# Where a stretch of 256 bytes begins: moving the transposed activations of a two-layer trunk by 128 bytes in SBUF

## The chip, the cores and the metric

The kernel runs on one core of one Trainium2 chip. The metric is the device time of one execution in microseconds (us), lower is better. The engines are named as the profile names them: PE is TensorE's matrix multiply, PEld its weight load, DVE is VectorE, ACT is ScalarE, POOL is GpSimd and SP is SyncE, whose queue issues most of the DMAs.

## The reference, cut to what matters

Two layers over 512 tokens of width 1024, in float32. Each layer is a mixer and a gated MLP, both with an RMS norm ahead and behind:

```python
for l in range(DEPTH):                         # 2
    h = rms_norm(x, norm_mix_pre[l])
    proj = h @ w_in[l]                         # 1024 x 2560
    ...                                        # attention, retention, pooling heads
    mix = jnp.concatenate([o_da, o_ret, o_pool], axis=-1) @ w_out[l]   # 1024 x 1024
    x = x + rms_norm(mix, norm_mix_post[l])
    h = rms_norm(x, norm_mlp_pre[l])
    y = conv_mlp(h, w_up[l], conv_w[l], conv_b[l], w_down[l])          # 1024 x 5632, 2816 x 1024
    x = x + rms_norm(y, norm_mlp_post[l])
```

## The kernel before

Every large product is computed from split operands. A float32 tile is written as a high part plus a low remainder, both in the type `float32r`, and each product is three matmuls: high by high, high by low and low by high. A matmul holds a 128x128 block as the stationary operand (loaded by a weight load of its own) and streams up to 512 columns of the other operand, the moving one, past it. In a row of the profile such as `ps_m<-ht,wb` the moving operand stands first and the stationary one second.

The weights come in units of 128x1024 elements: a DMA into a `raw` tile (three buffers), then a split by ACT (L272, L283) and DVE (L273, L284) into a pair `wa`, `wb` (six pairs) or, for the last units of a stage, into `space`, which is room of the tiles `U1` and `U2` that are free by then.

The activations are kept transposed, features on the partitions. The tile `ht` holds the transposed, split residual stream: 8 feature chunks, each with a high and a low row of 512 tokens, 32 KB in each partition. The tiles `c1`, `c2`, `c3h`, `c3l`, `c4h` and `c4l` (shown as `c`, `c3h` and so on) hold other split activations in the same manner: the mixer's output, and in the MLP a part of the gated values. `xs` is the residual stream itself, `cst` the constants, `par` the parameters of the layer.

A layer passes four stages, in this order on PE:

- In (w_in, five slices of 512 columns): in the first four, tokens are the output's rows, so the stationary operand is a block of `ht` and the moving one a weight tile (`wa,ht`). In the fifth, features are the rows: `ht` moves, the weights stand still (`ht,wa`). The attention and the retention are put in between by a table of due times, as short matmuls and transposes on the same PE.
- Out (w_out): stationary `c` tiles, moving weights (`wa,c`), still with retention and pooling in between.
- Up (w_up, eleven groups of four feature blocks): `ht` moves, weights stand still. The first group and part of the second are done in halves of 256 columns, the rest in full 512.
- Down (w_down, 22 chunks of 128 features, for each chunk 4 token blocks of 6 matmuls = 24 matmuls): weights move. The stationary operand is a `c` tile for chunks 0 to 7, `ht` (by then free for reuse) for chunks 8 to 15, and a `c` tile again for chunks 16 to 21.

By the loops, the matmuls of 512 columns that use `ht` number, in both layers together: 768 with `ht` standing and 192 with it moving in the In stage, 1872 with it moving in Up, 384 with it standing in Down. Another 480 in Up move 256 columns of `ht`.

Where the tiles lie: a pool gives the tiles of SBUF their bytes one behind the other, each tag at its first use. Ahead of the pools lie 16,384 bytes that are reserved and four small constants of 32 bytes each, so the first tile begins 128 bytes into a stretch of 256. The first is `cst`, then `xs`, `ht`, `par`, `rt` and the rest. Two lengths are rounded up by `up_to_lines`, those of `cst` and `par`:

```python
up_to_lines = lambda n: -(-n // 32) * 32
...
cst = one.tile([P, up_to_lines(NCONST)], F32, tag="cst", name="cst")
...
xs = one.tile([P, NT, D], F32, tag="xs", name="xs")
ht = one.tile([P, KC, 2, S], F32R, tag="ht", name="ht")
...
t = one.tile([P, up_to_lines(NPAR)], F32, tag="par", name=nm("par"))
```

`cst` gets 1152 words (4608 bytes, 18 stretches of 256) and `par` 480 words (1920 bytes, 7.5 stretches), so `cst`, `xs`, `ht` and `par` begin at byte 128 of a stretch, and every large tile behind `par` at byte 0. The lines that issue the matmuls and the transposes are two helpers, L319 (`mm`) and L322 (`tr`).

Of the kernel before, what the change touches and what calls it, by code (L numbers as in the profile page):

```python
# [11 lines left out]
F32 = mybir.dt.float32  # L12
# [8 lines left out]
P = 128  # L21
# [64 lines left out]
    _n += _w  # L86
NCONST = _n

up_to_lines = lambda n: -(-n // 32) * 32

_PAR_PARTS = [("gmix", 8), ("gmlp", 8), ("subln", 1), ("retn", 2), ("pools", 2), ("conv", 44 * 4), ("pw", 256)]
_PAR_AT = {}
# [44 lines left out]
def tile_trunk(ctx: ExitStack, tc: tile.TileContext, x, xt, win, wout, wup, wdown, gpost, par, lam, const, out):  # L137
# [3 lines left out]
    one = ctx.enter_context(tc.tile_pool(name="one", bufs=1))  # L141
# [10 lines left out]
    def nm(s):  # L152
        uid[0] += 1
        return f"{s}_{uid[0]}"
# [21 lines left out]
    def rot_tmp():  # L176
        return one.tile([P, 512], F32, tag="rt", name=nm("rt"))

    cst = one.tile([P, up_to_lines(NCONST)], F32, tag="cst", name="cst")
    def C(name):  # L180
        lo, hi = _CONST_AT[name]
        return cst[:, lo:hi]
# [954 lines left out]
```

## Time and profile before

| | |
|---|---|
| median of 3 runs | 1173.18 us (1172.22 to 1174.98) |
| the profiled execution's own time | 1173.23 us |
| its span, first to last instruction | 1171.4 us |
| PE busy | 1153.6 us (98%), 5472 matmuls |
| DVE busy, ACT busy | 742.1 us (63%), 549.1 us (47%) |
| mean granted TensorE clock | 0.999 |

The profiled execution stands 0.05 us from the median. Matmuls are pipelined, so that the duration in a matmul's row overlaps with the next matmul's. How fast PE works through a stage is read from the starts: the chain of work that ended last gives for each piece its start, its length from there to the next piece's start, and the number of instructions in it.

### The profile page before, as it was taken

Reading aid. Unit: us, or ns where it says so; the run is one execution under the profiler, and the core shown is the slowest. Engines: PE = TensorE matmul, PEld = TensorE weight load, DVE = VectorE, ACT = ScalarE, POOL = GpSimd, SP = SyncE. Lnnn points to the kernel's source line nnn. Section 1 sums busy time; section 2 is a strip of 40 time slices with the busy share of each in tenths; the row PEclk is TensorE's granted clock in tenths of the full one; section 3 lists DMA queues with packets and bytes.
Section 4 is the critical chain, followed back from the end, with each engine's and each line's share of the span. In section 5 each row is a group of like instructions: output and inputs, shape, how many; then the busy total and the mean of one; then the engine's idle time right before and its main releaser. Section 6 shows DMA issues by size and latency. Waiting matters only on the chain.

```text
span 1171.4 us, 14837 instructions
## 1 busy us (share of the span) xinstructions
PE 1153.6 (98%) x5472; PEld 945.5 (81%) x5472; DVE 742.1 (63%) x1668; ACT 549.1 (47%) x1049; POOL 12.5 (1%) x21
## 2 busy tenths in 40 slices
PE   9999999999999999999999999999999999999997
PEld 6788777988888888888888887789888888888885
DVE  5988696776556547422777896876856645663224
ACT  5966553564444335312467754454645434452211
POOL 1000000000000000000000000000000000000000
PEclk9999999999999999999999999999999999999999
DMA  8411131332222322324023111313332222223311
GB/s 316 132 60 64 55 104 45 109 126 90 97 102 76 105 91 100 105 90 144 1 96 120 56 66 42 108 40 121 113 103 93 85 96 97 102 74 107 98 46 55
DMA packets 31321, 109.22 MB, mean 93 GB/s; under 512 B 3729, under 2 KB 4241, under 8 KB 31249
## 3 DMA queue, kind: packets, MB, share of 16 engines
q1 hardware_dynamic: 29952, 105.12, 26.4%
q10 hardware_dynamic: 1296, 3.16, 0.8%
q8 instruction: 43, 0.70, 0.2%
q14 instruction: 30, 0.24, 0.1%
HBM read 106.16 MB, written 2.10 MB: 92 GB/s over the span
## 4 chain that ended last, share of the span: by engine, by line
PE 91%; DVE 4%; ACT 2%; DMA 2%; issue 1%; SPq 0%; DVEq 0%; ACTq 0%
PE ps_m L319 52%; PE ps_s L319 18%; PE ps_b L319 9%; PE ps_o L319 9%; PE ps_b L322 2%; DMA raw<-in_wout 1%; ACT t L686 1%; DMA raw<-in_wup 1%; ACT wa L283 0%; DVE space L284 0%; DVE ks L623 0%; DMA raw<-in_win 0%; PE ps_m L322 0%; DVE sm L378 0%; DVE wb L284 0%
## 5 line engine op out<-in xcount | busy, mean ns | idle before, releaser
L319 PE MATMUL ps_m<-ht,wb 128*128 128x512 f32 (+1 forms) x768 | 201.6, 371 | 0.0
L319 PE MATMUL ps_m<-ht,wa 128*128 128x512 f32 (+1 forms) x768 | 200.0, 368 | 0.0
L284 DVE SCALAR_TENSOR_TENSOR wa<-raw,par,wa 128x512 fp32r<-128x512 f32 x128 | 95.6, 747 | 157.4 <-ACT wa L283 157.2
L283 ACT ACTIVATE wa<-raw,par 128x512 fp32r<-128x512 f32 x128 | 92.1, 720 | 198.2 <-PE ps_m L319 97.9
L319 PEld LDWEIGHTS ps_m<-ht,wb 128*128 128x128 f32 x768 | 135.0, 188 | 26.7 <-issue 1.0
L319 PEld LDWEIGHTS ps_m<-ht,wa 128*128 128x128 f32 x768 | 135.1, 188 | 25.6 <-issue 1.0
L319 PE MATMUL ps_m<-wa,ht 128*128 128x512 f32 x512 | 151.4, 403 | 0.6 <-ACT wa L283 0.6
L319 PE MATMUL ps_m<-wb,ht 128*128 128x512 f32 x448 | 131.0, 398 | 0.0
L319 PEld LDWEIGHTS ps_m<-wa,ht 128*128 128x128 f32 x512 | 94.9, 191 | 21.5 <-ACT wa L283 1.5
L273 DVE TENSOR_TENSOR wb<-raw,wa 128x1024 fp32r<-128x1024 f32 x38 | 46.6, 1226 | 84.9 <-ACT wa L272 84.9
L284 DVE SCALAR_TENSOR_TENSOR wb<-raw,par,wb 128x512 fp32r<-128x512 f32 x128 | 95.6, 747 | 4.7 <-ACT wb L283 4.6
L319 PEld LDWEIGHTS ps_m<-wb,ht 128*128 128x128 f32 x448 | 82.8, 189 | 17.5
L283 ACT ACTIVATE wb<-raw,par 128x512 fp32r<-128x512 f32 x128 | 91.9, 720 | 4.1 <-PE ps_m L319 3.4
L272 ACT CAST wa<-raw 128x1024 fp32r<-128x1024 f32 x38 | 39.8, 1048 | 89.6 <-PE ps_m L319 81.3
L319 PE MATMUL ps_s<-ht,wb 128*128 128x512 f32 (+1 forms) x264 | 70.7, 376 | 0.0
L319 PE MATMUL ps_s<-ht,wa 128*128 128x512 f32 (+1 forms) x264 | 70.2, 374 | 0.0
L319 PE MATMUL ps_m<-wa,c 128*128 128x512 f32 x224 | 65.6, 399 | 1.3 <-DVE pooled L666 1.3
L319 PEld LDWEIGHTS ps_s<-ht,wb 128*128 128x128 f32 x264 | 47.3, 188 | 10.1
L319 PEld LDWEIGHTS ps_s<-ht,wa 128*128 128x128 f32 x264 | 47.6, 188 | 9.8
L319 PEld LDWEIGHTS ps_m<-wa,c 128*128 128x128 f32 x224 | 41.6, 188 | 11.3 <-DVE pooled L666 2.2
L686 ACT ACTIVATE t<-ps_s,sm 128x128 f32<-128x128 f32 (+3 forms) x64 | 33.5, 527 | 21.4 <-DVE sm L684 18.5
L1007 ACT ACTIVATE t<-ps_m,par 128x512 f32<-128x512 f32 x48 | 36.4, 772 | 12.9 <-PE ps_m L319 12.9
(314 smaller groups left out, 1888.1 us busy)
## 6 DMA issues: line engine op xcount, KB each, us to landing
raw<-in_wup SPq DMA_DIRECT2D x88, 512.0 KB, 3.4
raw<-in_wdown SPq DMA_DIRECT2D x44, 512.0 KB, 3.4
raw<-in_win SPq DMA_DIRECT2D x39, 512.0 KB, 3.7
raw<-in_wout SPq DMA_DIRECT2D x16, 512.0 KB, 3.5
xs<-in_x SPq DMA_DIRECT2D x4, 512.0 KB, 9.5
gain<-in_gpost ACTq DMA_DIRECT2D x4, 512.0 KB, 4.3
t<-in_xt SPq DMA_DIRECT2D x3, 512.0 KB, 6.8
out<-xs SPq DMA_DIRECT2D x4, 256.0 KB, 2.0
```

The source lines that it names most:

```text
L272: se.copy(h, r)
L273: ve.tensor_tensor(out=lo, in0=r, in1=h.bitcast(F32), op=ALU.subtract)
L283: se.activation(a, x, AF.Copy, scale=sc)
L284: ve.scalar_tensor_tensor(b, x, sc, a.bitcast(F32), op0=ALU.mult, op1=ALU.subtract)
L319: in_order(te.matmul(out, lhsT=lhsT, rhs=rhs, **k))
L322: in_order(te.transpose(out, in_, ident))
L686: se.activation(p[:, 0:n], sb[:, 0:n], AF.Exp, bias=top, accum_out=sums[:, m:m + 1])
L1007: se.activation(acc, ps, AF.Identity, bias=conv[:, f, 3:4], scale=conv[:, f, 2:3])
```

## The change

The unit of `up_to_lines` becomes 64 words (256 bytes), and ahead of `cst` a tile of 32 words (128 bytes) is placed that nothing reads or writes.

```diff
-up_to_lines = lambda n: -(-n // 32) * 32
+STRETCH = 64
+up_to_lines = lambda n: -(-n // STRETCH) * STRETCH
...
+    one.tile([P, STRETCH // 2], F32, tag="edge", name="edge")
     cst = one.tile([P, up_to_lines(NCONST)], F32, tag="cst", name="cst")
```

`par` becomes 512 words long; `cst` stays at 1152. The first byte of the tiles in each partition, from the built programs:

| tile | before | within 256 | after | within 256 |
|---|---|---|---|---|
| cst | 16512 | 128 | 16640 | 0 |
| xs | 21120 | 128 | 21248 | 0 |
| ht | 37504 | 128 | 37632 | 0 |
| par | 70272 | 128 | 70400 | 0 |
| rt | 72192 | 0 | 72448 | 0 |
| U1 (ks, act, space) | 74240 | 0 | 74496 | 0 |
| c1 | 107008 | 0 | 107264 | 0 |
| wa, the first | 141824 | 0 | 142080 | 0 |
| raw, the first | 190976 | 0 | 191232 | 0 |

Everything behind `par` moves by a whole 256 bytes. Each engine has the same instructions in the same order as before, with the same waits; the operands' addresses are all that differs. The program's DMAs are the same too.

## The prediction

> **What bounds the kernel now.** I read the page's busy times first, then the waits of PE, then the chain of work that ended last stage by stage, and last the groups of instructions within the stretches that the chain pointed to.
>
> ```profile
> PE 1153.6 (98%) x5472; PEld 945.5 (81%) x5472; DVE 742.1 (63%) x1668; ACT 549.1 (47%) x1049; POOL 12.5 (1%) x21
> PEclk9999999999999999999999999999999999999999
> PE 91%; DVE 4%; ACT 2%; DMA 2%; issue 1%; SPq 0%; DVEq 0%; ACTq 0%
> ```
>
> PE is busy for 98% of the span, the chain lies on it for 91%, and its granted clock is at the top all along. So the time goes with the interval from one matmul's start to the next. The waits of PE, in whole (total us, times, longest):
>
> ```profile
> PE ps_b L322 <- ACT t L702: 3.0, 4, 1.2
> PE ps_o L319 <- ACT t L491: 2.3, 1, 2.3
> PE ps_b L322 <- DVE ql L616: 1.4, 1, 1.4
> PE ps_m L319 <- DVE pooled L666: 1.3, 2, 0.7
> PE ps_m L319 <- ACT wa L283: 0.6, 1, 0.6
> PE ps_b L322 <- DVE ks L623: 0.5, 2, 0.3
> ```
>
> Eleven waits, 9.1 us together, none of them in Up or Down. There, the interval is all that counts, and it isn't the same everywhere. The Down stage has the cleanest comparison: the same line, the same plan (24 matmuls of 512 columns for each chunk of 128 features), the same moving weights; only the stationary tile differs. First the chain through chunks with a `c` tile, then through chunks with `ht` (start us, length us, instructions), and under each one of the groups from that stretch:
>
> ```profile
> 478.12 2.72 PE ps_m L319 x12
> 483.56 2.72 PE ps_m L319 x12
> 489.00 2.72 PE ps_m L319 x12
> 494.44 2.72 PE ps_m L319 x12
> 499.88 2.72 PE ps_m L319 x12
> ...
> L319 PE MATMUL ps_m<-wa,c 128*128 128x512 f32 x32 | 9.2, 389 | 0.0
> ```
>
> ```profile
> 521.99 2.79 PE ps_m L319 x12
> 527.57 2.79 PE ps_m L319 x12
> 533.15 2.79 PE ps_m L319 x12
> 538.72 2.79 PE ps_m L319 x12
> ...
> L319 PE MATMUL ps_m<-wa,ht 128*128 128x512 f32 x41 | 12.1, 395 | 0.0
> ```
>
> Each of these rows is half a chunk's work, and the next row starts a chunk later. With `c`, four chunks take 499.88 - 478.12 = 21.76 us for 96 matmuls: 226.7 ns each. With `ht`, three take 538.72 - 521.99 = 16.73 us for 72: 232.4 ns. No idle time stands in either group. `c` tiles begin at byte 0 of a stretch of 256, `ht` at 128; the weights begin at 0 in both. Now Up, where `ht` moves and the weights stand still:
>
> ```profile
> 262.90 22.40 PE ps_m L319 x96
> 307.70 22.40 PE ps_m L319 x96
> 352.50 22.40 PE ps_m L319 x96
> 397.30 22.40 PE ps_m L319 x96
> 442.10 22.40 PE ps_m L319 x96
> ...
> L319 PE MATMUL ps_m<-ht,wb 128*128 128x512 f32 x192 | 55.3, 396 | 0.0
> ```
>
> 22.40 us for 96 matmuls is 233.3 ns, in layer 0 as steady as a clock. So 226.7 where both operands begin at byte 0, 232.4 where the stationary one is off, 233.3 where the moving one is.
>
> **The change part by part.** It adds no instruction, no wait and no DMA, and moves none past another; the padding tile is never touched. What changes is the addresses. I price it as: every matmul that uses `ht` takes the interval of one that uses a `c` tile.
>
> Up, 512 columns: 233.3 - 226.7 = 6.6 ns by 1872 matmuls = 12.4 us. All of it is on the path, since PE waits for nothing there. The cover that must hold is the supply of weights:
>
> ```profile
> 247.00:467.00 220.00, 220.00 (x950) 177.28 (x950) 132.32 (x190) 101.97 (x151) 0.00 (x0) 1.00 0.28 96
> ```
>
> In this stretch (us, then busy us of PE, PEld, DVE, ACT and POOL, clock, DMA share, GB/s) PE is busy for all of 220 us, DVE for 132, ACT for 102, the DMA engines for 28%. A PE that is 3% faster raises DVE's share from 60% to 62%; nothing becomes late.
>
> Down, 512 columns: 232.4 - 226.7 = 5.7 ns by 384 = 2.2 us, by the same reading.
>
> In, 512 columns: here PE is interrupted by the attention's transposes and scores, and after an interruption even aligned matmuls are slow for a while. The Out stage shows that, whose operands all begin at byte 0 and which is interrupted by the retention in the same manner; its rows stand first, two rows of In behind them:
>
> ```profile
> 187.87 4.11 PE ps_m L319 x18
> 765.84 4.11 PE ps_m L319 x18
> ```
>
> ```profile
> 31.87 5.58 PE ps_m L319 x24
> 593.61 5.58 PE ps_m L319 x24
> ```
>
> 4.11 / 18 = 228.3 ns against 5.58 / 24 = 232.5 ns, a gain of 4.2 ns. Of the 768 matmuls with `ht` standing I count 720 (the first ones of layer 0 and those right behind a transpose keep their intervals): 3.0 us. The ends are 0 and 5.8 ns by 768 = 4.5 us. The 192 with `ht` moving, at 4 ns for 170 of them: 0.7 us, ends 0 and 1.3.
>
> Up, 256 columns: the chain's row for them, and the only matmuls of 256 columns with both operands at byte 0, three scores of the attention:
>
> ```profile
> 231.67 11.56 PE ps_m L319 x96
> ...
> 81.35 0.51 PE L319 MATMUL ps_s<-ks,c 128*128 128x256 f32 x3
> 81.70 0.28 PE L319 MATMUL ps_s<-ks,ql 128*128 128x256 f32 x1
> ```
>
> 11.56 / 96 = 120.4 ns, against (81.70 - 81.35) / 3 = 117 ns. That would be 3.4 ns by 480 = 1.6 us. Three matmuls are a thin row, and the disturbance costs might be fixed for each matmul with nothing left over here, so I take half, 0.8 us; ends 0 and 480 by (120.4 - 226.7 / 2) = 3.4 us.
>
> ACT and DVE, which write and read `ht`, `xs`, `cst` and `par`: priced at nothing, by the same line writing `ht` and `c`:
>
> ```profile
> L1069 DVE TENSOR_TENSOR ht<-act,ht 128x512 fp32r<-128x512 f32 x16 | 10.5, 685 | 0.0
> L1069 DVE TENSOR_TENSOR c<-act,c 128x512 fp32r<-128x512 f32 x12 | 8.3, 692 | 29.7 <-ACT c L1068 29.7
> L1068 ACT CAST ht<-act 128x512 fp32r<-128x512 f32 x16 | 9.1, 615 | 0.0
> L1068 ACT CAST c<-act 128x512 fp32r<-128x512 f32 x12 | 7.5, 624 | 42.5 <-PE ps_m L319 42.5
> ```
>
> 685 against 692 ns and 615 against 624: the tile at byte 128 is not the slower one. The transposes use the identity in `cst` as the moving operand and I expect nothing of them either; no row shows them with an aligned one.
>
> Given back: PE comes earlier to the eleven waits, while the ACT or DVE work that it waits for starts no more than a block of 24 matmuls earlier than it does now. 24 by 4.2 ns = 0.1 us, eleven times: 1.1 us lost at most. I take it whole.
>
> Sum: 12.4 + 2.2 + 3.0 + 0.7 + 0.8 - 1.1 = 18.0 us. The profiled execution took 1173.23 us, 0.05 above the median, so the forecast is 1173.2 - 18.0 = 1155.2, rounded to 1155 us. If all upper ends hold and nothing is given back: 12.4 + 2.2 + 4.5 + 1.3 + 3.4 = 23.8 us, 1149.4. If an aligned `ht` reaches only the disturbed interval of 228.3 ns: 5.0 by 1872 + 4.1 by 384 = 10.9 us, with 0 for In and the 256-column part and 1.1 given back: 1163.4.
>
> **The rivals.**
>
> Half a cure: only one side answers to the address. If `ht` as the moving operand stays at 233.3 ns (its cost would then come from being read 512 columns long as a tile that ACT and DVE also touch), there remain 2.2 + 3.0 - 1.1 = 4.1 us, 1169 us. If the stationary side stays, 12.4 + 0.7 + 0.8 = 13.9 us, 1159. For it speaks that no row shows an aligned activation as the moving operand in a long run; against it that weights at byte 0 do move at 226.7.
>
> No change: what slows the matmuls with `ht` is not byte 128 but where the tile lies in SBUF, 37 to 70 KB into a partition, or its being one of 32 KB. The tile stays there after the change, and the time would be 1173. Against it: `c` tiles spread over 103 to 140 KB and moving weights in `U1` from 74 KB on (those of the row at 187.87) run at 226.7 to 228.3, so place has not mattered elsewhere. The Trainium skill speaks for this rival: SBUF — State Buffer, Specifications, gives lines of 16 bytes as the only unit of access, and TensorE: Matmul & The Clock Gate, Step-by-step, has the moving operand and the weight load read through two independent ports. By that, byte 128 is as good as byte 0 and the time stays; the 5.7 ns between the two stretches of Down are what it doesn't explain.
>
> Slower: the stretch that counts is one of 512 bytes, not 256. Before, every large tile but the four begins at byte 0 of 512 too (`c1` 107008 = 209 by 512, the first `wa` 141824 = 277 by 512). After, all of them begin at byte 256 of 512, `ht` included (37632 = 73 by 512 + 256). Then the aligned matmuls of Down and Out, 8 + 6 chunks of 24 in Down and 8 of 24 in Out, in two layers 1056, would rise by 5.7 ns: 6.0 us slower, 1179, with `ht` no better than now. It decides if byte 256 is as bad as byte 128; no tile in this trace begins there, so nothing speaks against it but that a half of 512 is the less likely unit. If only the distance between the two operands counts, this rival falls, since all distances become multiples of 256.
>
> **How the numbers follow.** Full effect 0.75, half a cure 0.11, no change 0.07, slower 0.07. A change of under 0.2% (2.3 us) can't be told from none here. Faster: 0.75 + 0.11 = 0.86; same 0.07; slower 0.07. The range reaches down to the upper ends, 1150, and up through 1163.4 into half a cure, 1167; that leaves out no change, slower, and the far half of half a cure.
>
> **What would show it.** In the changed kernel's chain, Up's rows of 96 matmuls take 21.8 us instead of 22.40, and Down's chunks with `ht` 2.72 in the half instead of 2.79; rows with `c` stay at 2.72. The mean of `ps_m<-wa,ht` in that stretch falls from 395 to 389. In's blocks of 24 fall from 5.58 to about 5.48. PE's busy time falls by about 18 us, its waits grow by about one. If the `c` rows rise to 2.79 the stretch is 512; if only one kind of `ht` row falls it is half a cure; if none does, place and not phase is the cause. What would make me wrong by a little is In, where I have disturbed rows alone.

## The result, and the profile after

The changed kernel takes 1156.57 us in the median of four executions, against 1173.37 us for the kernel before beside it: ratio 0.9851, 95% interval 0.9832 to 0.9871. The forecast was 1155 us, in a range of 1150 to 1167. One of the four, the profiled one, ran at a mean granted clock of 0.752 and took 1422.05 us, so the ratio rests on the other three (1154.94 to 1156.71 us), and the profile shown here is that of a further run of the same kernel (the first experiment), at 0.998.

The head of its page:

```profile
span 1155.2 us, 14837 instructions
...
PE 1137.0 (98%) x5472; PEld 944.7 (82%) x5472; DVE 740.5 (64%) x1668; ACT 547.7 (47%) x1049; POOL 12.5 (1%) x21
```

The span fell by 16.2 us, PE's busy time by 16.6, and the share of 98% stayed. DVE and ACT did the same work in almost the same time. The chain of work that ended last, in order of time (start us, length us, instructions): a row of Out, Up's halves, Up, Down with `c` (476 and 492 us), Down with `ht` (514 us), and a row of layer 1's In:

```profile
186.92 4.12 PE ps_m L322 x18
...
230.74 11.55 PE ps_m L322 x96
...
261.53 21.76 PE ps_m L322 x96
...
476.41 2.72 PE ps_m L322 x12
...
492.73 2.72 PE ps_m L322 x12
...
514.49 2.72 PE ps_m L322 x12
...
591.52 5.49 PE ps_m L322 x24
```

Up's 96 matmuls take 21.76 us instead of 22.40: 226.7 ns each, to the tenth what the `c` rows took. Down's chunks can't be told apart any more: 2.72 before and after the change of tile at about 500 us. In's blocks of 24 fell from 5.58 to 5.49. Up's halves stand where they were, 11.55 against 11.56. The groups of instructions in the two stretches, Down with `ht` and Up:

```profile
L322 PE MATMUL ps_m<-wa,ht 128*128 128x512 f32 x41 | 11.9, 389 | 0.0
...
L322 PE MATMUL ps_m<-ht,wb 128*128 128x512 f32 x192 | 53.9, 389 | 0.0
```

The mean of one went from 395 and 396 ns to the 389 that the `c` rows had. The waits of PE:

```profile
PE ps_b L325 <- ACT t L705: 2.9, 4, 1.2
PE ps_o L322 <- ACT t L494: 2.3, 1, 2.3
PE ps_b L325 <- DVE ql L619: 1.5, 1, 1.5
PE ps_m L322 <- DVE pooled L669: 1.3, 2, 0.7
PE ps_b L325 <- DVE ks L626: 0.6, 2, 0.4
PE ps_m L322 <- ACT wa L286: 0.5, 1, 0.5
PE ps_b L325 <- DVE sm L385: 0.3, 2, 0.2
PE ps_b L322 <- DVE t L808: 0.2, 1, 0.2
PE ps_m L322 <- DVE ht L506: 0.2, 1, 0.2
PE ps_b L325 <- ACT t L410: 0.2, 1, 0.2
```

10.0 us against 9.1: the four smallest rows are new, and 0.9 us was given back.

### The profile page after: what moved, and what is told of

Read it like the earlier page. It is cut to its first block, busy times and chain, and to the rows that moved or that the text cites. A ratio compares the mean times of both kernels' runs of the same rounds, so it can differ in the third digit from the quotient of the medians.

```text
span 1420.3 us, 14837 instructions
## 1 busy us (share of the span) xinstructions
PE 1406.6 (99%) x5472; PEld 1021.5 (72%) x5472; DVE 752.8 (53%) x1668; ACT 558.3 (39%) x1049; POOL 12.5 (1%) x21
## 4 chain that ended last, share of the span: by engine, by line
PE 98%; DVE 1%; ACT 1%; issue 0%; DMA 0%; SPq 0%; DVEq 0%; ACTq 0%
PE ps_m L322 56%; PE ps_s L322 19%; PE ps_b L322 10%; PE ps_o L322 10%; PE ps_b L325 2%; PE ps_m L325 0%; ACT t L689 0%; PE ps_s L325 0%; DMA raw<-in_win 0%; ACT t L705 0%; PE ps_o L325 0%; DVE pooled L669 0%; DVE t L770 0%; DVE t L821 0%; ACT c L616 0%
## 5 line engine op out<-in xcount | busy, mean ns | idle before, releaser
L322 PE MATMUL ps_m<-ht,wb 128*128 128x512 f32 (+1 forms) x768 | 238.4, 425 | 0.0
L322 PE MATMUL ps_m<-ht,wa 128*128 128x512 f32 (+1 forms) x768 | 237.5, 423 | 0.0
L322 PEld LDWEIGHTS ps_m<-ht,wa 128*128 128x128 f32 x768 | 145.7, 204 | 48.6 <-issue 1.5
L322 PEld LDWEIGHTS ps_m<-ht,wb 128*128 128x128 f32 x768 | 145.9, 204 | 48.3 <-issue 1.4
L322 PE MATMUL ps_m<-wa,ht 128*128 128x512 f32 x512 | 178.1, 462 | 0.1
L322 PE MATMUL ps_m<-wb,ht 128*128 128x512 f32 x448 | 156.0, 460 | 0.0
L322 PE MATMUL ps_s<-ht,wb 128*128 128x512 f32 (+1 forms) x264 | 83.4, 431 | 0.0
L322 PE MATMUL ps_s<-ht,wa 128*128 128x512 f32 (+1 forms) x264 | 83.1, 429 | 0.0
L322 PE MATMUL ps_m<-wa,c 128*128 128x512 f32 x224 | 79.1, 466 | 0.5 <-DVE pooled L669 0.5
L322 PE MATMUL ps_m<-wb,c 128*128 128x512 f32 x112 | 43.7, 477 | 0.0
```

Source lines behind the costliest of these rows:

```text
L322: in_order(te.matmul(out, lhsT=lhsT, rhs=rhs, **k))
```

## The experiments

The first four ran beside each other, against 1172.08 us for the kernel before (1169.6 to 1173.31); the next four, on another chip, beside 1170.89 us (1169.85 to 1172.24); the last four beside 1171.5 us (1169.66 to 1174.08).

### e1: the change once more

No edit.

> The changed kernel once more, for a profile at the full TensorE clock. Theory (each operand's own first byte within 256 decides): about 1156 us, Up's chain rows of 96 matmuls 21.8 us instead of 22.40, Down's half chunks with ht 2.72 instead of 2.79, rows with c tiles at 2.72. Rival (part of the gain comes from xs, cst or par): the PE rows account for clearly less than the whole difference of 17 us. Rival (a stretch of 512 counts): rows with c rise to 2.79.

Measured: 1156.73 us, ratio 0.9874 (0.986 to 0.9889). The rows are those above. In this kernel every large tile begins at byte 256 of a stretch of 512, and the rows with `c` stayed at 2.72, so the rival of the 512 stretch is out.

### e2: only ht moved

```diff
+    one.tile([P, 32], F32, tag="pad", name="pad")
     ht = one.tile([P, KC, 2, S], F32R, tag="ht", name="ht")
...
-        t = one.tile([P, up_to_lines(NPAR)], F32, tag="par", name=nm("par"))
+        t = one.tile([P, 512], F32, tag="par", name=nm("par"))
```

(against the kernel before; `par`, which lies right behind `ht`, moves with it)

> Only ht goes to byte 0 (128 bytes of padding ahead of ht instead of ahead of cst); cst and xs stay at byte 128. Theory (only the matmuls' operands count): as fast as the changed kernel, 1156 us within 2. Rival (xs and cst, read by ACT, DVE and the transposes, bring a part): the part by which it falls short, above 2 us.

Measured: 1156.54 us, ratio 0.9869 (0.9854 to 0.9883). The whole gain comes with `ht` and `par`, of which the matmuls of Up and Down read `ht` alone; `cst` and `xs`, which ACT, DVE and the transposes read, bring nothing that shows.

### e3: only ht put back

```diff
     one.tile([P, STRETCH // 2], F32, tag="edge", name="edge")
...
+    one.tile([P, 32], F32, tag="pad", name="pad")
     ht = one.tile([P, KC, 2, S], F32R, tag="ht", name="ht")
...
-        t = one.tile([P, up_to_lines(NPAR)], F32, tag="par", name=nm("par"))
+        t = one.tile([P, 480], F32, tag="par", name=nm("par"))
```

(against the changed kernel, as all that follow but e4)

> The changed kernel with ht and par put back to byte 128, cst and xs stay at 0. Theory (only the matmuls' operands count): the whole gain is gone, 1173 us within 2, Up's rows at 22.40. Rival (xs and cst bring a part): under 1171.

Measured: 1172.38 us, ratio to the kernel before 1.0003 (0.9993 to 1.0013). The whole gain is gone. The chain has Up and Down back where they were:

```profile
263.05 22.40 PE ps_m L323 x96
...
500.04 2.72 PE ps_m L323 x12
...
516.58 2.78 PE ps_m L323 x12
```

### e4: everything at byte 128

```diff
-        t = one.tile([P, up_to_lines(NPAR)], F32, tag="par", name=nm("par"))
+        t = one.tile([P, 512], F32, tag="par", name=nm("par"))
```

(against the kernel before: no padding ahead of `cst`, so that the whole stack of tiles keeps its offset of 128)

> Every large tile begins at byte 128 of 256, weights and c tiles too. Theory A (each operand's own first byte counts): every matmul of 512 columns is slow, also the 1056 with c tiles, 5.7 ns more each on top of the time before: 1179 us or more. Theory B (only the distance between the moving and the stationary operand counts, within 256): all distances are 0 again, as fast as the changed kernel, 1156 us, Up's rows at 21.8.

Measured: 1156.06 us, ratio 0.987 (0.9856 to 0.9885). This is the experiment that decided. No large tile begins at byte 0 here, and the kernel is as fast as the changed one:

```profile
261.04 21.76 PE ps_m L319 x96
...
492.24 2.72 PE ps_m L319 x12
...
514.00 2.72 PE ps_m L319 x12
```

Up, Down with `c` and Down with `ht` all run at 226.7 ns. Theory A falls, and with it the prediction's reading of the rows. What counts is how far the moving operand's first byte lies from the stationary one's. (Within a tile, the blocks that a matmul of 512 columns reads begin at multiples of 512 bytes, so the tiles' first bytes give the difference within 256.)

### e5: the weights at byte 128, ht and c at 0

```diff
     wp = ctx.enter_context(tc.tile_pool(name="wp", bufs=1))
+    wp.tile([P, 32], F32, tag="wpad", name="wpad")
```

> The changed kernel with 128 bytes of padding behind the weight tiles' pool opening, so that wa, wb and the pools behind them begin at byte 128, ht and the c tiles at byte 0. Theory B (the distance between the moving and the stationary operand, within 256, counts): the matmuls with ht are as slow as in the kernel before, and those with c tiles slow too, 1056 by 5.7 ns: 1173 + 6 = 1179 us, Down's half chunks 2.79 with c and with ht. Rival (ht has to be at the same place as c, the weights don't count): 1156 us.

Measured: 1175.91 us, ratio to the kernel before 1.004 (1.0025 to 1.0055).

```profile
306.74 22.31 PE ps_m L323 x96
...
488.09 2.80 PE ps_m L323 x12
...
521.69 2.80 PE ps_m L323 x12
```

The `c` tiles, never moved, became slow because the weights did: 2.80 for 12 where they had 2.72. So the rival falls. The edit moves `wa` and `wb` alone. The last three units of Out and of Down lie in `space`, room of `U1` and `U2` that stays at byte 0, so their matmuls with `c` keep a difference of 0. They nearly kept their pace too (the mean ns of one stands ahead of the last bar; the same two groups had 399 and 392 in the kernel before):

```profile
L323 PE MATMUL ps_m<-wa,c 128*128 128x512 f32 x224 | 66.7, 403 | 1.3 <-DVE pooled L670 1.3
L323 PE MATMUL ps_m<-space,c 128*128 128x512 f32 x96 | 23.3, 392 | 0.0
```

So 768 matmuls with `c` could lose, and not the 1056 that the expectation counted. By the mean of the intervals under 250 ns, those with `wa` or `wb` moving rose from 226.9 to 232.8 ns in Down and from 228.4 to 232.9 in Out, and those with `space` from 227.1 to 228.3 and from 228.6 to 229.4: together 4.5 us. In return Up's mean fell from 233.32 to 232.85 ns, 0.9 us. That leaves 3.6 us, while the medians differ by 5.0, with a 95% interval from 2.9 to 6.4, and 6 was expected. (The 1173 from which the expected 1179 starts is another session's; beside this run the kernel before took 1170.89.)

The difference is 128 here for every matmul that uses moved weights, and yet a stretch settles at one of two values, 232.4 or 233.3 ns. In layer 0, Up runs at 22.31 and Down at 2.80 (5.60 from chunk to chunk); in layer 1 it is the other way round, and Down's chunks come every 5.57 us:

```profile
842.43 22.40 PE ps_m L323 x96
...
1102.59 2.78 PE ps_m L323 x12
```

What chooses between the two isn't shown.

### e6, e7 and e8: ht at 64, at 192 and at 256

```diff
+    one.tile([P, 16], F32, tag="pad", name="pad")
     ht = one.tile([P, KC, 2, S], F32R, tag="ht", name="ht")
...
-        t = one.tile([P, up_to_lines(NPAR)], F32, tag="par", name=nm("par"))
+        t = one.tile([P, 496], F32, tag="par", name=nm("par"))
```

(e6; e7 has 48 and 464 words, e8 64 and 576 and in `small` a padded shape of 8 words instead of 16)

> ht and par begin at byte 64, all else as in the changed kernel (distance 64). If any distance but 0 costs: about 1172 us. If only 128 costs (two halves of 256 that answer to different operands): 1156 us. In between if the cost grows with the distance.

> ht and par begin at byte 192 (distance 192, or -64). If the cost depends on the size of the distance alone: the same as with byte 64. If it is a matter of which operand runs ahead: different from byte 64, one near 1156 and one near 1172 or above.

> ht begins at byte 0 of 512, all tiles behind it at byte 256 of 512 (distance 256; the small tiles are 32 instead of 64 bytes long to make room). If the period is 256: as fast as the changed kernel, 1156 us. If it is 512 and distances of a half are bad: 1172 us or more.

Measured: e6 1164.42 us, ratio 0.9938 (0.9924 to 0.9953); e7 1168.52 us, 0.9977 (0.9966 to 0.9987); e8 1156.44 us, 0.9872 (0.9858 to 0.9887). The chains, Up and then Down with `ht`, of e6:

```profile
305.93 21.97 PE ps_m L323 x96
...
522.89 2.80 PE ps_m L323 x12
```

of e7:

```profile
231.13 10.98 PE ps_m L323 x96
...
306.43 22.40 PE ps_m L323 x96
...
525.99 2.75 PE ps_m L323 x12
```

and of e8:

```profile
304.73 21.76 PE ps_m L323 x96
...
525.04 2.72 PE ps_m L323 x12
```

Count the difference as moving minus stationary, within 256. In e6 it is 64 in Up (21.97, 228.9 ns) and 192 in Down (2.80, 233.3 ns); in e7 it is 192 in Up (22.40, 233.3 ns) and 64 in Down (2.75, 228.9 ns). The two operands' roles are exchanged and the intervals go with the signed difference: which operand is ahead does matter. A difference of 256 is as good as 0, so I count differences within 256. The row at 231.13 is the last part of Up's halves: its 256-column matmuls take 10.98 us for 96, 114.4 ns, instead of 11.56. The short matmuls gain from the very difference that costs the long ones.

### e9: the low rows apart from the high ones

```diff
-    ht = one.tile([P, KC, 2, S], F32R, tag="ht", name="ht")
-    hth, htl = ht[:, :, 0, :], ht[:, :, 1, :]
+    ht = one.tile([P, 2 * KC * S + 32], F32R, tag="ht", name="ht")
+    hth, htl = (ht[:, o:o + KC * S].rearrange("p (k s) -> p k s", k=KC) for o in (0, KC * S + 32))
...
-        t = one.tile([P, up_to_lines(NPAR)], F32, tag="par", name=nm("par"))
+        t = one.tile([P, 480], F32, tag="par", name=nm("par"))
```

> The high rows of ht begin at byte 0 of 256, the low rows (a tile half of their own) at byte 128. In Down each chunk and token block runs six matmuls with the stationary rows high, high, high, high, low, low, and the moving weights are always at 0. Theory P (the operands of the matmul itself count): the intervals of the fifth and sixth are the long ones. Theory L (what counts is the moving operand against the weight load that runs beside it, that of the next matmul): the fourth and fifth are long, and the sixth isn't. In both, Up and Down lie between 226.7 and 233.3 ns on the mean, and the time is 1160 to 1166 us.

Measured, one run: 1165.0 us. The first matmuls with `ht` in Down, behind undisturbed ones with `c`, in the timeline of PE (start us, us, instructions at the end of the row):

```profile
502.80 0.62 PE L322 MATMUL ps_s<-wa,ht 128*128 128x512 f32 x2
503.25 0.62 PE L322 MATMUL ps_s<-wb,ht 128*128 128x512 f32 x2
503.71 0.64 PE L322 MATMUL ps_s<-wa,ht 128*128 128x512 f32 x2
504.19 0.40 PE L322 MATMUL ps_b<-wa,ht 128*128 128x512 f32 x1
```

The pairs are high, high and low; from start to start they take 0.45, 0.46 and 0.48 us. One by one the starts give 227, 227, 226, 233, 241 and 240 ns, and in layer 1 227, 226, 227, 232, 241 and 240. The fourth, whose own operands are both at 0, is already 6 ns longer: beside it runs the weight load of the fifth, from byte 128. That speaks for theory L. The kernel before shows the same at its own border in Down: the last matmul with `c`, both operands at 0, takes 233 and 232 ns in the two layers, behind others of 226 and 227. So a matmul's own operands (theory P) are not the whole account. But in e9 the sixth is long too, which L did not expect, and the intervals behind it never come to rest (they repeat only with the chunk); in the kernel before, the first `c` matmul behind the last with `ht` still takes 231 ns. A disturbance outlasts the matmul that causes it, so what passes from one matmul to the next stays open.

### e10, e11 and e12: ht at 32, at 96 and at 16

```diff
+    one.tile([P, 8], F32, tag="pad", name="pad")
     ht = one.tile([P, KC, 2, S], F32R, tag="ht", name="ht")
...
-        t = one.tile([P, up_to_lines(NPAR)], F32, tag="par", name=nm("par"))
+        t = one.tile([P, 504], F32, tag="par", name=nm("par"))
```

(e10; e11 has 24 and 488 words; e12 takes `ht` as a view that begins 4 words into a tile 8 words longer, with 504 words for `par`)

> ht and par begin at byte 32. The moving minus the stationary operand's byte within 256 is then 32 in Up and 224 in Down and In. Measured so far, interval per matmul: 226.7 ns at 0, 228.9 at 64, 232.4 to 233.3 at 128, 233.3 at 192. Sawtooth (the cost grows from 0 up and falls back at 256): Up about 227.8, Down 233.3 or more, about 1162 us. Bump (highest about 160): Up about 227.3, Down about 230, about 1160 us. Alignment alone (only a multiple of 64 or 128 matters): both as with 64, 1164 us.

> ht and par begin at byte 96: the moving minus the stationary byte is 96 in Up, 160 in Down and In. Both the sawtooth and the bump: Up about 231, Down about 233, about 1169 us. Alignment alone: not between the values for 64 and 128.

> ht begins at byte 16, par at 32: the difference is 16 in Up, 240 in Down and In. Sawtooth: Up about 227.2, Down 233.3 or more, about 1161 us. Bump: Up about 227, Down about 228, 1157 to 1158 us. If differences within 32 bytes don't count: 1156.5 us, both at 226.7.

Measured: e10 1171.9 us, ratio 1.0004 (0.9994 to 1.0014); e11 1174.22 us, 1.002 (1.001 to 1.003); e12 1165.99 us, 0.9955 (0.9941 to 0.9969). Up and Down with `ht` of e10:

```profile
306.55 22.40 PE ps_m L323 x96
...
526.49 2.80 PE ps_m L323 x12
```

of e11:

```profile
307.98 22.40 PE ps_m L323 x96
...
528.02 2.81 PE ps_m L323 x12
```

and of e12:

```profile
307.12 22.24 PE ps_m L323 x96
...
525.41 2.72 PE ps_m L323 x12
```

All three theories of the shape missed. At 32 the cost is full, not a small part of it as the sawtooth and the bump had it; at 16 it is 5.0 ns; at 64 only 2.2. At 240 it is nothing in Down, but not everywhere: In's blocks of 24 with `ht` standing have the same difference in e12, and some of them run at 226.7 ns, others at 233.3:

```profile
584.41 5.44 PE ps_m L323 x24
590.73 5.60 PE ps_m L323 x24
...
603.23 5.45 PE ps_m L323 x24
```

Over all of In, the mean of the intervals under 250 ns with `ht` standing is 232.1 there, against 229.1 at a difference of 0 (e1). Intervals of undisturbed 512-column matmuls by the difference, moving minus stationary, within 256 bytes (chain rows divided by their counts; in Down, the starts of successive chunks; "or" where stretches with the same difference settled at two values):

| difference | 0 | 16 | 32 | 64 | 96 | 128 | 160 | 192 | 224 | 240 |
|---|---|---|---|---|---|---|---|---|---|---|
| ns | 226.7 | 231.7 | 233.3 | 228.9 | 233.3 | 232.4 or 233.3 | 234.3 | 233.3 | 233.3 | 226.7 or 233.3 |
| read from | e1, e4, e8 | e12 Up | e10 Up | e6 Up, e7 Down | e11 Up | before, e3, e5 | e11 Down | e7 Up, e6 Down | e10 Down | e12 Down, e12 In |

No difference that was tried beats 0 for 512 columns, so the changed kernel stays the best version.

## Why the prediction was right, and where its reason was not

The price was right: it came from rows in which the operands lay to each other as they would lie after. The terms, with the starts of the chain's rows before and after:

- Up, 512 columns: forecast 12.4 us. 22.40 - 21.76 = 0.64 us for 96, that is 6.7 ns by 1872 = 12.5 us.
- Down: forecast 2.2 us. 2.79 - 2.72 in the half chunk, with 32 half chunks of `ht` in two layers: 2.2 us.
- Up, 256 columns: forecast 0.8 us. Nothing: 11.55 us against 11.56. The three scores at 117 ns were no measure; the right end of the bound was 0. In e7, at a difference of 192, the short matmuls are faster than at 0 (114.4 ns).
- In: forecast 3.0 + 0.7 us, with 1.1 given back. The quiet blocks gained 5.58 - 5.49 = 0.09 us, 3.8 ns by matmul instead of 4.2. The mean of In's intervals under 250 ns fell by 3.3 ns with `ht` standing (232.4 to 229.1) and by 1.6 with it moving (232.3 to 230.7): 3.3 by 710 = 2.3 us and 1.6 by 160 = 0.3. The waits took 0.9 of it. That leaves 1.7 us where I had 2.6.

12.5 + 2.2 + 0 + 1.7 = 16.4 us, and the span fell by 16.2. So nearly all of the 1.8 us between the 18.0 forecast and this lie in the 256-column term (0.8) and In (0.9). In's mean fell by less than its quiet blocks because the first intervals behind an interruption gain nothing: with `ht` standing, the second to the fourth take 231.8 ns before and 231.9 after, while those from the twelfth on fall from 232.3 to 226.9. The prediction named this, but counted 720 of the 768 matmuls at the full 4.2 ns.

The step that failed is the reading "226.7 where both operands begin at byte 0, 232.4 where the stationary one is off, 233.3 where the moving one is". The trace showed one offset (0) for nearly all tiles and another for `ht`, so "begins at 0" and "begins where the other operand begins" could not be told apart in it. e4 tells them apart: all at 128 is as good as all at 0. For this change both readings give the same time, so the number came out right whichever of them holds; that the wrong one did no harm is luck. The name of the change, a stretch of 256 at whose byte 0 tiles begin, has the same flaw. The prediction had the second reading in half a sentence, as the reason for which the rival of the 512 stretch would fall, and did not see that it overturned the main one too.

Of the rivals, place is out (e3 and e8 leave `ht` where it is in SBUF to within 256 bytes, and one loses all and the other keeps all), half a cure is out (Up and Down both fell to 226.7), the 512 stretch is out (e1, e8). By the Trainium skill's lines of 16 bytes alone (SBUF — State Buffer, Specifications), differences of 16, 32 and 64 bytes, all whole lines, would be as good as 0; the runs don't agree, with 231.7, 233.3 and 228.9 ns against 226.7. The Trainium skill also says of TensorE's two independent read ports that loading the next weights takes no read bandwidth from the running matmul (TensorE: Matmul & The Clock Gate, Step-by-step); here the interval depends on the two operands' addresses together, by up to 7.6 ns of 226.7, so the two reads are not without effect on one another. Why 64 is mild and 32 is not, and why 240 is free in one stretch and not in the next, no run here shows.

## What to carry to other kernels

Where PE is busy all along, read the interval from start to start in the chain of work for each kind of operand, not only the mean duration in a group: two stretches of the same line with different intervals are worth a search. In a kernel like this one, let the moving and the stationary operands begin at the same byte within 256; whether that byte is 0 or 128 made no difference, and the spare tile cost 128 bytes in each partition and no time. And when a trace holds one odd tile among even ones, test "everything odd" before believing that odd is bad.

## What was not expected of the hardware

The interval of a float32r matmul of 512 columns, each with its own weight load, depends on the difference of the operands' first bytes within 256: 226.7 ns at 0 and 256, 234.3 at the worst, with a mild place at 64 (228.9) between two of 233.3. The direction counts: 64 takes 228.9 and 192, as far the other way, 233.3, whichever operand is `ht`.

It isn't a fixed price by matmul. In the kernel before, the starts in Up alternate between about 229 and 237 ns, and those of Down with `ht` repeat every seven matmuls, between 228 and 241, while the plan repeats every three and every six. And stretches with the same difference can settle at two values, 232.4 or 233.3 at 128 (e5) and 226.7 or 233.3 at 240 (e12). At 0, every long stretch came to 226.7.

Matmuls of 256 columns answer otherwise: 114.4 ns in the last part of e7's halves at a difference of 192, 120.3 at 0 (e1). In the two operations on ACT and DVE that were compared, nothing shows: DVE's subtraction into `ht` took 685 ns from byte 128 and 683 from byte 0, ACT's cast 615 and 616.

```profile
L1072 DVE TENSOR_TENSOR ht<-act,ht 128x512 fp32r<-128x512 f32 x16 | 10.4, 683 | 0.0
L1071 ACT CAST ht<-act 128x512 fp32r<-128x512 f32 x16 | 9.1, 616 | 0.0
```
